# Three dilations of an attention phase taken in another order, and stores issued on a second DMA queue

## The chip, the cores and the metric

The kernel runs on one core of one Trainium2 chip. The metric is the device time of one execution in microseconds (us); three executions give a median of 2603.55 us, from 2603.17 to 2605.61 us.

## What is computed

The reference is a trunk of two layers over 1024 tokens of width 1024. Each layer is a mixer with a residual, then a SwiGLU feed-forward block with a residual. The change touches only the mixer of the second layer, `mixer_cd`, which has two kinds of heads side by side:

```python
hq, hf, hi, hg, sq, sk, sv = split_cols(h @ w_in, CD_SPLITS)
o_c = hgrn2_recurrence(silu(hq), k_in, hi, log_f)          # 4 heads, chunkwise recurrence
o_c = rms_norm(o_c, norm_g) * sigmoid(hg)
sq, sk = rope(sq, pos), rope(sk, pos)                      # 3 patterns x 4 heads
for p, (window, dilation) in enumerate(((128, 1), (512, 4), (2048, 16))):
    o_p, lse_p = dilated_window_attention(sq[:, :, p], sk[:, :, p], sv[:, :, p], window, dilation)
wts = softmax(stack(lses))                                 # over the three patterns
o_d = sum over p of o_p * wts_p
return concat([o_c, o_d]) @ w_out
```

So each of the four attention heads has three outputs, one per pattern, and they are combined with weights from their softmax sums. In the code and below the patterns are p = 0, 1, 2 (dilations 1, 4, 16), and "dilation p" is the one of pattern p.

## The kernel before, in words

All matrix products in 32 bits are made of three products of a high and a low half (`mm3`, L123). TensorE (PE) runs them nearly without a break; everything else is arranged around PE's order of instructions, which inside `mixer_cd` is the order of the program text (`manual_schedule`, L2216). The order on the other engines and on SyncE's DMA queue (SP) is set by the compiler's scheduler, which goes by its own estimate of when each instruction is ready. Each queue works strictly in its order once it is set.

The phase has a main stream of projections: `hgrn_v` (values of the recurrence, twice 8 row tiles), `swa_v(p)` (values of dilation p, for all heads), `swa_qk` (queries and keys of dilation 1, one head), `hgrn_gates` (twice 4 tiles), and `leading` (nine pieces of the output projection, of six matmuls each, that need only the first six of eight inputs). Queries and keys of the dilations 0 and 2 were projected in an earlier phase and lie in DRAM (`pairs.qk`), not yet turned by rope.

Between pieces of the main stream `tick(cost)` (L2195) puts in steps of two other generators: it adds cost times a rate to a counter for each and runs one step for each full unit. `hgrn_v` costs 1 per tile, `swa_v` 16 in all, `swa_qk` 8, `hgrn_gates` 8 per half, `leading` 0.5 per piece. `chain` is the recurrence (rate 0.7). `local` (L2153) is the attention: a unit `Attend(h, p)` has four steps n, each of two blocks of 128 queries. One call of `local` does `scores` of step n, `flip` (transposes) of the step before and `outputs` of the one before that, so a unit's results are complete two calls after its last scores. Its softmax lies on VectorE (DVE) and ScalarE (ACT), L2017 and L2018.

The order before is: `swa_v(1)`; `swa_qk` of heads 0 and 1; `hgrn_v` second half; `swa_qk` 2 and 3; `swa_v(2)`; `swa_v(0)`; gates; leading. Units of dilation 1 become ready after each `swa_qk` (rate 0.7), the four of dilation 2 only after `swa_v(2)`, the four of dilation 0 only after `swa_v(0)`, both at rate 1.0 (L2225 to L2228):

```python
for p in (2, 0):
    swa_v(p, tick)
    ready += [(h, p, None) for h in range(4)]
    rate[0] = 1.0
```

A unit of dilation 0 or 2 is set up one unit ahead (`load`, L1960): k and q come in from DRAM, a second copy `rs` with the halves of the head exchanged comes in by two DMAs each (L1986, L1987), and four turns of three DVE operations on 128x512 (`part`, L1967) do the rope. The table of cosines is loaded by `turn` (L1898), and again for dilation 0. For dilation 1 the rope follows the projection directly (L1923, L1924) and frees its PSUM bank.

Values go from PSUM through an ACT copy to the tile `sw` and by SP to DRAM (`scr_v`, L1885; `scr_h`, L1700); scaled outputs of the recurrence go to `scr_g` (L1833). All DMAs are on SP. Outputs of the dilations 1 and 2 go to `scr_o`. When a unit of dilation 0 ends a group g of four blocks, `combine` (L2096) loads the other two (`cm`, L2101), mixes the three on DVE and ACT, and two calls of `local` later transposes the result on PE (L2131) and stores it to `cat` (L2134). The output projection after the phase loads `cat` again (`cin`, L1084) and splits it into halves; the leading pieces lack the inputs 6 and 7 of `cat[0]`, which are the attention heads 2 and 3.

## Time and profile before

| | before |
|---|---|
| median of 3 executions | 2603.55 us |
| the profiled execution, its own time | 2600.88 us |
| its span in the profile | 2599.1 us |
| PE busy | 2555.1 us, 98% |
| DVE busy | 1662.7 us, 64% |
| ACT busy | 1033.5 us, 40% |
| DMA, share of 16 engines in hardware queues | 53.3% |
| granted clock of PE, mean | 0.996 |

The profile counts PE as busy while a matmul runs, and matmuls overlap; so what matters for this kernel is the little time in which PE is not busy, what ended each such wait, and the stretches in which PE was granted less than its full clock. Times within the span are given as us from its start; `mixer_cd` lies between about 1390 and 1875 us.

### The profile page before, as it was taken

The page shows a single profiled execution, that of the slowest core. Times are in us where ns is not written, and L with a number is a line of the kernel's source. Part 1 is how long each engine was busy: PE and PEld are TensorE (multiplying, and loading weights), DVE is VectorE, ACT ScalarE, POOL GpSimd, SP SyncE. Part 2 cuts the span into 40 slices and gives each one's busy share as a digit, 9 for nine tenths or more (in the row PEclk, how much of TensorE's full clock was granted, in tenths as well). Part 3 has the DMA queues.
Part 4 walks back from the last instruction along what each step waited for, and adds up shares of the span by engine and source line. Part 5 has one row for each costly group of instructions (what it writes and reads, how often), then busy time and mean ns, then how long its engine had stood idle before and what let it go on. Part 6 is the DMA issues. An engine that isn't in the chain of part 4 may idle for free. (4 is left out here: it accounts for less than half of the span.)

```text
span 2599.1 us, 37598 instructions
## 1 busy us (share of the span) xinstructions
PE 2555.1 (98%) x14179; PEld 2129.6 (82%) x14179; DVE 1662.7 (64%) x2814; ACT 1033.5 (40%) x1855; POOL 514.4 (20%) x440
## 2 busy tenths in 40 slices
PE   8999999999999999999999999998999999999998
PEld 6888888888888888888888898877788888888887
DVE  7887776585656665567665457567767565566554
ACT  5432123343333344344443555454544333334442
POOL 1110121334342300024330000000023433331001
PEclk9999999999999999999999999999999999999999
DMA  4434446424556688533326424578762555668853
GB/s 143 137 100 151 123 144 202 167 84 167 176 190 203 222 284 289 193 126 121 132 98 196 125 90 111 153 187 230 244 216 68 172 177 196 205 209 279 275 183 120
DMA packets 279510, 447.63 MB, mean 172 GB/s; under 512 B 49152, under 2 KB 140064, under 8 KB 279200
## 3 DMA queue, kind: packets, MB, share of 16 engines
q1 hardware_dynamic: 279328, 445.23, 53.3%
q8 instruction: 111, 1.82, 0.3%
q14 instruction: 71, 0.58, 0.1%
HBM read 307.16 MB, written 137.97 MB: 171 GB/s over the span
## 5 line engine op out<-in xcount | busy, mean ns | idle before, releaser
L103 DVE TENSOR_TENSOR w<-raw,w 128x1024 fp32r<-128x1024 f32 (+1 forms) x319 | 381.5, 1198 | 155.8 <-ACT w L102 155.0
L102 ACT CAST w<-raw 128x1024 fp32r<-128x1024 f32 (+1 forms) x319 | 306.8, 963 | 280.8 <-PE psu L128 140.4
L126 PE MATMUL psu<-hnh,w 128*128 128x512 f32 x888 | 355.3, 400 | 7.3 <-ACT w L102 7.3
L128 PE MATMUL psu<-hnh,w 128*128 128x512 f32 x888 | 347.8, 392 | 0.0
L127 PE MATMUL psu<-hnl,w 128*128 128x512 f32 x888 | 347.6, 391 | 0.0
L126 PEld LDWEIGHTS psu<-hnh,w 128*128 128x128 f32 x888 | 167.7, 189 | 41.4 <-ACT w L102 7.7
L128 PEld LDWEIGHTS psu<-hnh,w 128*128 128x128 f32 x888 | 167.4, 189 | 36.3 <-DVE w L103 0.8
L127 PEld LDWEIGHTS psu<-hnl,w 128*128 128x128 f32 x888 | 167.8, 189 | 33.9 <-DVE hnl L2253 0.6
L187 POOL TENSOR_TENSOR acc<-acc,sq 128x512 f32<-128x512 f32 x48 | 69.7, 1453 | 517.4 <-ACT sq L183 400.2
L302 POOL TENSOR_TENSOR ws<-raw 128x512 f32<-128x512 f32 x50 | 73.9, 1478 | 421.5 <-DMA raw<-in_dram 232.2
L103 DVE TENSOR_TENSOR w<-ws,w 128x1024 fp32r<-128x1024 f32 x47 | 61.7, 1313 | 118.5 <-ACT w L102 118.5
L103 DVE TENSOR_TENSOR hidq<-hr,hidq 128x1024 fp32r<-128x1024 f32 x72 | 82.1, 1141 | 76.0 <-ACT hidq L102 75.5
L102 ACT CAST hidq<-hr 128x1024 fp32r<-128x1024 f32 x72 | 70.2, 979 | 100.0 <-DMA hr<-ts 61.1
L126 PE MATMUL psm<-hidq,w 128*128 128x512 f32 (+1 forms) x275 | 106.0, 385 | 0.0
L127 PE MATMUL psm<-hidq,w 128*128 128x512 f32 (+1 forms) x275 | 105.8, 385 | 0.0
L128 PE MATMUL psm<-hidq,w 128*128 128x512 f32 (+1 forms) x275 | 105.8, 385 | 0.0
L126 PE MATMUL psu<-t3h,w 128*128 128x512 f32 x224 | 87.3, 390 | 1.0 <-ACT u L365 1.0
L126 PE MATMUL psu<-t4h,w 128*128 128x512 f32 x224 | 87.5, 391 | 0.5 <-ACT c L372 0.5
L128 PE MATMUL psu<-t4h,w 128*128 128x512 f32 x224 | 87.2, 389 | 0.0
L127 PE MATMUL psu<-t4l,w 128*128 128x512 f32 x224 | 87.2, 389 | 0.0
L127 PE MATMUL psu<-t3l,w 128*128 128x512 f32 x224 | 87.1, 389 | 0.0
L128 PE MATMUL psu<-t3h,w 128*128 128x512 f32 x224 | 87.1, 389 | 0.0
(489 smaller groups left out, 6476.8 us busy)
## 6 DMA issues: line engine op xcount, KB each, us to landing
raw<-in_dram SPq DMA_DIRECT2D x227, 512.0 KB, 4.0
sd<-in_dram SPq DMA_DIRECT2D x44, 512.0 KB, 3.9
hid<-hid SPq DMA_DIRECT2D x88, 256.0 KB, 2.7
sd<-sd SPq DMA_DIRECT2D x44, 512.0 KB, 3.3
hr<-ts SPq DMA_DIRECT2D x40, 512.0 KB, 4.9
raw<-sd SPq DMA_DIRECT2D x40, 512.0 KB, 4.2
hd<-h SPq DMA_DIRECT2D x48, 256.0 KB, 3.5
h<-hd SPq DMA_DIRECT2D x48, 256.0 KB, 5.6
```

The source lines that it names most:

```text
L102: S.copy(hi, src)
L103: eng.tensor_tensor(lo, src, hi.bitcast(F32), op=SUB)
L126: T.matmul(o, lh, rh, start=first and i == 0, stop=False, **kw)
L127: T.matmul(o, lh, rl, start=False, stop=False, **kw)
L128: T.matmul(o, ll, rh, start=False, stop=last and i == n - 1, **kw)
L187: (eng or G).tensor_tensor(a, a, q, op=ADD)
L302: G.tensor_tensor(s[:, HT:], b[:, :HT], b[:, HT:], op=ADD)
```

## The change

The units are taken in another order. The values are projected in the order `swa_v(2)`, `swa_v(1)`, `swa_v(0)`; units of dilation 2 are ready from the start, `swa_qk` of head 0 stands before `swa_v(0)` and those of heads 1 to 3 behind it, with units of dilation 0 between them. The rate of `local` is 0.47 from the second `hgrn_v` on and 0.68 after `swa_v(0)`; that of `chain` is 0.72. A third generator, `turns` (rate 0.38), does the rope of dilation 0 in 16 items of half a head's q or k: it loads, turns and stores to new DRAM tensors `final`, from which the units of dilation 0 load q and k ready-made. Units of dilation 2 load their exchanged copies one quarter at a time, from a ring of four half-size tiles `rs`. As a head's dilation 0 can now end before its dilation 1, its output may go to `scr_o` too, and `combine` then loads all three. A counter `made` keeps the units and the head being projected within the two buffers of q and of k. Stores of `scr_h`, `scr_v`, `scr_g` and of the combined outputs to `cat` are issued on ACT's DMA queue (`store`).

The diff, cut:

```diff
@@ -56,6 +56,7 @@
...
+    store = nc.scalar.dma_start
...
@@ -1651,7 +1652,7 @@
...
-        scr_o = dr.tile([4, 2, T_LEN, 132], F32, name="scr_o")
+        scr_o = dr.tile([4, 3, T_LEN, 132], F32, name="scr_o")
...
@@ -1697,7 +1698,7 @@
                 def put(tt, o):
...
-                    dma(scr_h[tt * P:(tt + 1) * P, pair * 256:(pair + 1) * 256], t)
+                    store(scr_h[tt * P:(tt + 1) * P, pair * 256:(pair + 1) * 256], t)
...
@@ -1830,7 +1831,7 @@
...
-                    dma(scr_g[half, h].rearrange("p (c t) -> p c t", c=4), go)
+                    store(scr_g[half, h].rearrange("p (c t) -> p c t", c=4), go)
...
@@ -1868,8 +1869,7 @@
...
-            def swa_v(p, tick):
+            def swa_v(p, tick, groups):
...
@@ -1882,9 +1882,9 @@
                 def put(tt, o):
...
-                    dma(scr_v[p][tt * P:(tt + 1) * P, :], vs)
-                for tts in ((0, 1, 2), (3,), (4,), (5, 6, 7)):
+                    store(scr_v[p][tt * P:(tt + 1) * P, :], vs)
+                for tts in groups:
...
@@ -1893,22 +1893,52 @@
...
-            table = {}
-            def turn(p):
-                if (p == 0) not in table:
-                    table.clear()
-                    t = table[p == 0] = tl("turn", (2, T_LEN))
-                    if p:
-                        dma(t[:, :, 0:320], c_rope[:, :, T_LEN:])
-                    else:
-                        dma(t, c_rope[:, :, 0:T_LEN])
-                return table[p == 0]
+            turn12 = tl("turn12", (2, 320))
+            dma(turn12, c_rope[:, :, T_LEN:])
+            final = [dr.tile([2, P, 2, HT], F32, name=f"fin{h}") for h in range(4)]
+            def exchanged(i, b, src):
+                x = tl("rs", bufs=4)
+                dma(x[0:64], src[i, 64:128, b])
+                dma(x[64:128], src[i, 0:64, b])
+                return x
+            def rotated(c, x, cos, sin):
+                V.tensor_tensor(x, x, sin, op=MULT)
+                V.tensor_tensor(c, c, cos, op=MULT)
+                V.tensor_tensor(c, c, x, op=ADD)
+            def turns():
+                prepare()
+                for _ in range(4):
+                    yield
+                    ahead[0].turn(1)
+                items = [(h, i) for h in range(4) for i in range(2)]
+                for half in range(NH):
+                    t = tl("turn0", (2, HT))
+                    dma(t, c_rope[:, :, half * HT:(half + 1) * HT])
+                    held = {}
+                    def load(n):
+                        if n < len(items):
+                            h, i = items[n]
+                            c = tl("rs", bufs=4)
+                            dma(c, pairs.qk[0, h][i, :, half])
+                            held[n] = c, exchanged(i, half, pairs.qk[0, h])
+                    load(0)
+                    for n, (h, i) in enumerate(items):
+                        load(n + 1)
+                        c, x = held.pop(n)
+                        rotated(c, x, t[:, 0], t[:, 1])
+                        dma(final[h][i, :, half], c)
+                        yield
...
             def swa_qk(h, tick):
...
-                w, turns = wload(("cd", 20 + h), ("cd", 32 + h)), turn(1)
+                w = wload(("cd", 20 + h), ("cd", 32 + h))
...
@@ -1947,45 +1977,49 @@
...
                 def __init__(self, h, p, qk):
...
-                    self.todo = []
+                    self.todo, self.asks = [], []
                     if p == 1:
...
                     else:
-                        self.load(turn(p), pairs.qk[p, h])
-                    self.vp = values(h, p)
+                        self.load(pairs.qk[p, h])
+                    self.vp = None
...
-                def load(self, turns, src):
+                def load(self, src):
...
+                    if self.p == 0:
+                        dma(self.k, final[self.h][1])
+                        dma(self.q, final[self.h][0])
+                        return
...
                     def streams(ap):
-                        return ap.rearrange("p (s i) -> p s i", s=16) if self.p else ap
-                    def part(c, x, b):
-                        for y, t in ((x, 1), (c, 0)):
-                            if self.p:
-                                t = turns[:, t, None, 256 + b * 32:288 + b * 32].to_broadcast([P, 16, 32])
-                            else:
-                                t = turns[:, t, b * HT:(b + 1) * HT]
-                            V.tensor_tensor(y, y, t, op=MULT)
-                        V.tensor_tensor(c, c, x, op=ADD)
-                    for i, t in ((1, self.k), (0, self.q)):
-                        if self.p and i == 0:
-                            c4 = t.rearrange("p b t -> p (b t)").rearrange("p (s b i) -> p b s i", s=16, b=2)
-                            cs = [c4[:, b] for b in range(2)]
-                            for b in range(2):
-                                dma(cs[b], src[i, :, b].rearrange("p (s i) -> p s i", s=16))
-                        else:
-                            cs = [streams(t[:, b]) for b in range(2)]
-                            dma(t, src[i])
-                        x = tl("rs", (2, HT), 2)
-                        dma(x[0:64], src[i, 64:128])
-                        dma(x[64:128], src[i, 0:64])
-                        self.todo += [lambda c=cs[b], y=streams(x[:, b]), b=b: part(c, y, b) for b in range(2)]
+                        return ap.rearrange("p (s i) -> p s i", s=16)
+                    def ask(c, i, b):
+                        x = streams(exchanged(i, b, src))
+                        cos, sin = (turn12[:, t, None, 256 + b * 32:288 + b * 32].to_broadcast([P, 16, 32])
+                                    for t in range(2))
+                        self.todo.append(lambda: rotated(c, x, cos, sin))
+                    c4 = self.q.rearrange("p b t -> p (b t)").rearrange("p (s b i) -> p b s i", s=16, b=2)
+                    dma(self.k, src[1])
+                    for b in range(2):
+                        dma(c4[:, b], src[0, :, b].rearrange("p (s i) -> p s i", s=16))
+                    for i, cs in ((1, [streams(self.k[:, b]) for b in range(2)]), (0, [c4[:, b] for b in range(2)])):
+                        self.asks += [lambda c=cs[b], i=i, b=b: ask(c, i, b) for b in range(2)]
+                    for _ in range(2):
+                        self.asks.pop(0)()
+                def turn(self, n):
+                    for _ in range(n):
+                        if self.todo:
+                            self.todo.pop(0)()
+                        if self.asks:
+                            self.asks.pop(0)()
...
@@ -2075,11 +2109,16 @@
...
-                    if p == 0:
-                        late.append(combine(h, g, ol, sums))
+                    ended.add((h, p, g))
+                    if p == 0 and (h, 1, 1) in ended:
+                        late.append(combine(h, g, (ol, sums)))
...
-                    if p == 1:
+                    if p == 0:
+                        V.tensor_copy(ol[:, :, P:w], sums)
+                        dma(scr_o[h, 2, g * HT:(g + 1) * HT].rearrange("(j i) d -> i j d", i=P)[:, :, 0:w],
+                            ol[:, :, 0:w])
+                    elif p == 1:
...
@@ -2092,11 +2131,16 @@
...
-            def combine(h, g, ol, sums):
-                t, st = [ol], [sums]
-                for p in range(2):
+                    if p == 1 and g and (h, 0, 1) in ended:
+                        late.extend(combine(h, i) for i in range(2))
+            def combine(h, g, own=None):
+                if own is None:
+                    for _ in range(1 + 2 * g):
+                        yield
+                t, st = ([own[0]], [own[1]]) if own else ([], [])
+                for p in range(2) if own else (2, 0, 1):
...
@@ -2131,7 +2175,7 @@
...
-                dma(catd[g][4 + h], go)
+                store(catd[g][4 + h], go)
...
@@ -2148,34 +2192,34 @@
...
-            ready, late, diag, holding, combined = [], [], [], [0], [0]
+            ready, late, diag, holding, combined, made, ended = [], [], [], [0], [0], [0], set()
+            unit, ahead = [], []
+            def prepare():
+                if ready and not ahead and len(unit) // 2 + made[0] < 2:
+                    ahead.append(Attend(*ready.pop(0)))
...
             def local():
...
-                line, now, ahead = [None, None], [], []
-                def prepare():
-                    if ready and not ahead:
-                        ahead.append(Attend(*ready.pop(0)))
+                line = [None, None]
                 while True:
                     nxt = None
+                    now = unit
...
-                    if now and ahead and now[1] > 1:
-                        for turn_part in ahead[0].todo[:2]:
-                            turn_part()
-                        del ahead[0].todo[:2]
+                    if now and ahead and now[1]:
+                        ahead[0].turn(now[1] // 3 + 1)
...
-                        for turn_part in ahead[0].todo:
-                            turn_part()
+                        ahead[0].turn(4)
...
+                        now[0].vp = values(now[0].h, now[0].p)
...
                     if now:
                         nxt = tuple(now)
...
-                            now = []
+                            now.clear()
...
@@ -2188,13 +2232,13 @@
...
-            hg_chain, loc = chain(), local()
-            works = (loc, hg_chain)
-            due, rate = [0.0] * 2, [0.0, 0.7]
+            hg_chain, loc, turner = chain(), local(), turns()
+            works = (loc, hg_chain, turner)
+            due, rate = [0.0] * 3, [0.0, 0.72, 0.38]
...
             def tick(cost):
...
-                for i in range(2):
+                for i in range(3):
...
@@ -2202,12 +2246,16 @@
...
+            tokens = (0, 1, 2), (3,), (4,), (5, 6, 7)
             def query_keys(hs):
...
-                    while len(ready) + holding[0] > 1:
+                    while holding[0] > 1:
...
-                    ready.append((h, 1, swa_qk(h, tick)))
-                    rate[0] = 0.7
+                    made[0] = 1
+                    qk = swa_qk(h, tick)
+                    made[0] = 0
+                    ready.insert(0, (h, 1, qk))
...
@@ -2215,17 +2263,24 @@
...
+                ready += [(h, 2, None) for h in range(4)]
+                next(turner)
...
-                swa_v(1, tick)
-                query_keys((0, 1))
+                rate[1] = 0.72
+                swa_v(2, tick, tokens)
+                rate[0] = 0.47
...
-                query_keys((2, 3))
-                for p in (2, 0):
-                    swa_v(p, tick)
-                    ready += [(h, p, None) for h in range(4)]
-                    rate[0] = 1.0
+                swa_v(1, tick, tokens)
+                query_keys((0,))
+                swa_v(0, tick, tokens)
+                for _ in turner:
+                    pass
+                ready += [(h, 0, None) for h in range(2)]
+                rate[0] = 0.68
+                query_keys((1, 2, 3))
+                ready += [(h, 0, None) for h in (2, 3)]
...
```

## Rows read from the trace of the kernel before

**Rows 1.** Windows of five stretches: us, busy time of each engine, granted clock, DMA share, GB/s.

```profile
core 0: us, PE busy (x) PEld busy (x) DVE busy (x) ACT busy (x) POOL busy (x), PEclk, DMA share, GB/s
1390.00:1624.00 234.00, 231.64 (x2352) 202.89 (x2350) 127.96 (x319) 115.08 (x306) 5.31 (x5) 1.00 0.42 120
1624.00:1633.30 9.30, 6.35 (x141) 4.82 (x140) 4.99 (x11) 1.47 (x6) 0.00 (x0) 0.63 0.70 172
...
1759.00:1773.30 14.30, 7.66 (x31) 6.16 (x31) 7.34 (x21) 3.04 (x14) 1.01 (x1) 0.76 0.93 210
1773.30:1870.00 96.70, 89.53 (x497) 74.56 (x496) 78.13 (x293) 51.64 (x145) 0.00 (x0) 1.00 0.79 235
...
sum 510.00, PE 488.23 PEld 414.75 DVE 310.88 ACT 250.72 POOL 14.91; mean PE 69.75 PEld 59.25 DVE 44.41 ACT 35.82 POOL 2.13
```

**Rows 2.** Waits of PE, 1390 to 1900: us in total, times, longest us.

```profile
PE psm L2011 <- issue: 6.6, 1, 6.6
PE psu L2131 <- DVE ol L2124: 3.1, 4, 2.0
PE psu L126 <- DVE k L1924: 2.9, 1, 2.9
PE psm L2011 <- DVE k L1924: 2.4, 2, 1.8
PE psm L2043 <- ACT e L1832: 1.7, 1, 1.7
PE psm L2058 <- DVE pt L2060: 1.2, 1, 1.2
PE psm L2058 <- DVE w L2119: 1.2, 1, 1.2
PE psm L2011 <- DVE stat L2017: 1.1, 1, 1.1
```

**Rows 3.** Timeline of PE at 1769: start us, us, instruction, idle before it.

```profile
1768.94 1.62 PE L2011 MATMUL psm<-k,q 128*128 128x128 f32 x4 [6.64 <-issue]
```

**Rows 4.** Timeline of DVE at 1621 to 1627 and at 1767.

```profile
1621.31 1.28 DVE L1973 TENSOR_TENSOR q<-q,turn 128x512 f32<-128x512 f32 x2
...
1626.06 1.02 DVE L1924 TENSOR_TENSOR k<-psu,sw 128x512 f32<-128x512 f32 x1
...
1766.94 1.29 DVE L1973 TENSOR_TENSOR rs<-rs,turn 128x512 f32<-128x512 f32 x2 [3.12 <-DMA rs<-qk]
```

**Rows 5.** Timeline of SP at 1761.

```profile
1760.91 0.56 SPq L1885 DMA_DIRECT2D scr_v<-sw  x1
1761.52 0.48 SPq L1987 DMA_DIRECT2D rs<-qk  x1
```

**Rows 6.** Waits of SP, 1390 to 1900: us in total, times, longest us.

```profile
SPq L1885 <- ACT sw L1884: 55.5, 18, 11.4
```

**Rows 7.** DMA issues, 1390 to 1900: count, KB each, median us to landing.

```profile
raw<-in_dram SPq DMA_DIRECT2D x33, 512.0 KB, 4.5
rs<-qk SPq DMA_DIRECT2D x32, 256.0 KB, 4.7
```

**Rows 8.** Line L1885: ns min/median/max of the issue, first and last start.

```profile
L1885 SPq DMA_DIRECT2D scr_v<-sw x24: 319/320/2715, 1428.9 to 1760.9; - x24
```

**Rows 9.** Timeline of PE at the phase's end.

```profile
1861.40 0.59 PE L2131 MATMUL psu<-cf,ol 128*128 128x128 f32 x2 [0.47 <-DVE ol L2124]
...
1869.98 0.30 PE L2131 MATMUL psu<-cf,ol 128*128 128x128 f32 x1 [1.98 <-DVE ol L2124]
...
1874.17 0.39 PE L127 MATMUL psg<-hnl,w 128*128 128x512 f32 x1
```

**Rows 10.** Timeline of SP at the phase's end.

```profile
1863.16 0.33 SPq L2134 DMA_DIRECT2D cat<-sw  x1
1866.85 1.78 SPq L1084 DMA_DIRECT2D cin<-cat  x4
```

**Rows 11.** Timeline of DVE at the phase's end.

```profile
1871.06 1.29 DVE L103 TENSOR_TENSOR hnl<-cin,hnh 128x512 fp32r<-128x512 f32 x2
```

More of the change, by code (lines that the diff above doesn't have):

```diff
@@ L1922, in swa_qk @@
                         for y, t in ((x3, 1), (o3, 0)):
-                            V.tensor_tensor(y, y, turns[:, t, half * P:(half + 1) * P, None].to_broadcast([P, P, 4]), op=MULT)
+                            V.tensor_tensor(y, y, turn12[:, t, half * P:(half + 1) * P, None].to_broadcast([P, P, 4]), op=MULT)
                         V.tensor_tensor(z[:, half].rearrange("p (r i) -> p i r", r=4), o3, x3, op=ADD)
```

## The prediction, made before the change was timed

> **What bounds the kernel now.** I read the stages first, then PE's waits, then the timeline around each long wait, engine by engine, until something was found that had really been late. In the windows [rows 1] PE is busy 488.2 of the 510.0 us that hold the phase; the 21.8 us in which it is not, and two stretches of low clock, are all that this change can touch, because it leaves every matmul in place. In 1624 to 1633 the granted clock is 0.63 and in 1759 to 1773 it is 0.76: full speed but for some 6.9 us at half speed (1.2 instead of 2.4 GHz), each worth 9.3 x 0.37 = 14.3 x 0.24 = 3.4 us. Both follow a long wait of PE, of 2.9 and 6.6 us [rows 2]; no wait of 2 us or less has such a stretch behind it. So the most there is to win is 21.8 + 6.8 = 28.6 us, or 1.1%. Waits [rows 2] sort into five places: (A) first scores of a dilation 1 unit waiting for its rope, 2.4; (B) `swa_v(2)` wanting three PSUM banks while rope of the last `swa_qk` still holds one, 2.9; (C) units of dilation 2, whose steps come so close that the flip waits for the softmax, 1.7 and three small ones, 2.6 in all; (D) the first scores of dilation 0, 6.6; (E) waits on DVE in the gates, 1.2 + 1.2 + 1.1 and small ones, 4.1; (F) transposes of the last combines, 2.0 + 0.5.
>
> D is put down to "issue", so I followed it back. PE starts at 1768.94 [rows 3]; DVE had waited 3.1 us for the exchanged copy of q and taken it at 1766.94 [rows 4]. SP had issued that copy only at 1761.52, right behind the store of a value tile at 1760.91 [rows 5]. SP works in order, and that store waits for ACT's copy of a bank that PE had just finished. Over the phase SP waited 55.5 us in 18 such places [rows 6].
>
> **The change part by part.** *The order of steps.* I walked the ticks through both versions. Before, `swa_v(0)`, gates and leading give 16 + 16 + 4.5 = 36.5 ticks at rate 1.0 for eight units: 32 calls, 2 to finish the last outputs, 2 for its combine, 36 in all. After, 48 ticks at 0.47 (22.6 calls) hold the four units of dilation 2 and the first of dilation 1; `swa_qk` 1 to 3, gates and leading give 24 + 16 + 4.5 = 44.5 ticks at 0.68, 30.3 calls, for seven units, which want 28 + 4 = 32. The last combine therefore runs past the end of leading.
>
> *A.* Heads 0 to 2 of dilation 1 now start 9 to 20 us after their projection. Head 3 starts one gate piece behind it, the cover that before gave waits of up to 1.8. I keep 1.5 of 2.4: gain 0.9 (bounds 0 and 2.4).
>
> *B.* `swa_v` behind `swa_qk` is still there, once. Before, DVE had just spent 2.6 us on q of a dilation 2 unit (four operations, two of them shown) before it came to the rope that PE wanted, done at 1626.06 + 1.02 [rows 4]. After, the rope of dilation 2 is over by then and at most one item of `turns` (3 x 0.64 = 1.9 us) can stand there. Without it PE would wait some 0.5 us, with it up to 2.4; I keep about 1.2 of the wait and one chance in six of the low clock: 6.3 - 1.8 = 4.5 (bounds 0 and 6.3).
>
> *C.* At 0.47 no two calls are adjacent, except the two that `query_keys` forces ahead of head 0. Those two wait as the worst pairs before did: I keep 2.0 of 2.6, gain 0.6.
>
> *D.* Units of dilation 0 have no rope, no table and no `rs` any more; two loads of 512 KB, 4.5 us each to landing for that size [rows 7], come from `final`, whose last store lies some 60 us earlier. Both loads can go out while `swa_v(0)` runs, since the value stores are no longer ahead of them on SP. I keep 0.5 of 6.6 + 3.4: gain 9.5 (bounds: 10.0, and 3 if the loads go out only with the unit).
>
> *E.* DVE is 81% busy in 1773 to 1870 78.1 of 96.7, [rows 1]. From these 96.7 us go rope for three units (36 operations of 0.64, 23 us) and some of the combines, which spread over 175 us: below 65%. Part of that load goes to the stretch of `swa_qk` 1 to 3. I keep 2.0 of 4.1: gain 2.1 (bounds 0 and 4.1).
>
> *F, the price.* From the transposes of the last head's first group to its input being split for the output projection there are 10.3 us: transposes at 1861.40 [rows 9], store at 1863.16 and reload at 1866.85 [rows 10], low half done by 1871.06 + 0.64 [rows 11]. Six leading pieces lay in between, and the first matmul after them, at 1874.17 [rows 9], had no wait. By the walk only two pieces are left behind those transposes. PE then has 2 x 1.4 us of leading, 2.1 us of matmuls with input 6 (nine), and 1.4 us of transposes: 6.3 us. It waits 10.3 - 6.3 = 4.0 us instead of 2.5, and with 4 chances in 10 of a low clock (3.4) the loss is 1.5 + 1.4 = 2.9 (bounds 0 and 7.5).
>
> *The stores.* 56 of them move. SP's issue takes 0.32 us [rows 8]; if ACT's costs the same it is 17.9 us on an engine that is busy 250.7 of 510 [rows 1], so it need not show. The worst place is behind a group of three value tiles, where the third copy comes 0.64 us later, six times: 3.8 us at most, nothing at least, as a bank is wanted only in turn. I take 0.3. The trace of before has no DMA on ACT.
>
> *What is added.* The 16 items move 16 x 3 x 256 KB = 12.6 MB, and the units load 4.2 MB where they loaded 8.4: 8.4 MB more, with some 64 more DMA issues on SP (against 56 fewer). Most falls in 1390 to 1624, where DMA is 42% busy at 120 GB/s; 21 MB more there with the rope loads of dilation 2 makes it about 73%, less than the 79% of the gates now [rows 1]. The DVE work is the same 16 x 3 operations. What I can't see is how SP's order copes with a ring of four `rs` tiles that `turns` and the units share: a load that waits for its tile holds up the weights behind it. Bounds 0 and 10; with the stores' 0.3 I take 2.7, nearer the lower end, because that stretch waited only 2.4 us of 234 so far.
>
> **Sum:** 0.9 + 4.5 + 0.6 + 9.5 + 2.1 - 2.9 - 2.7 = 12.0 us. The profiled execution's own 2600.88 becomes 2588.9; it was 2.7 us below the median, so the median goes from 2603.55 to about **2591**. A difference of 0.2%, 5.2 us, is about what a measurement of this kernel can tell from none.
>
> **A rule against the stores.** The rows show SP held for 55.5 us by copies that were not ready [rows 6], which is waiting in order and no transfer. The Trainium skill ("DMA: Bandwidth & Descriptors", section "Issuing engines are not separate DMA queues") says that DMAs of all issuing engines run on the same 16 DMA engines, so that a second issuing engine saves only the time of initiating. By that rule the moved stores would give nothing that PE sees; the trace so far speaks for the waiting.
>
> **The rivals.**
> - *The stores do not matter* (chance 0.09). What makes the loads of the first unit of dilation 0 late is the transfer and their place in the program, directly before the scores, and not the stores ahead of them on SP. D then gives 2 instead of 9.5: 2599. For it: the DMA engines are 93% busy in 1759 to 1773 [rows 1]; against it: the issue at 1761.52 is itself late [rows 5]. This is what the rule of the Trainium skill comes to here.
> - *The waits only move* (0.14). B stays whole (4.5 lost), the end waits 4 us longer still and surely falls to the low clock (2.0 above the 1.4 counted): 2591 + 10.5 = 2601.5, no change that can be measured. For it: the cover at the end really shrinks from six pieces to two; against it: D has a cause that is gone.
> - *Slower: the ring of `rs` holds SP, and SP the weights* (0.11). Each start of `swa_v(1)`, `swa_qk` 0 and `swa_v(0)` lies within the run of `turns`. If a weight load waits there until DVE has turned an item, PE waits for landing (4.5, [rows 7]) and, as at 1627, runs on at half clock (3.4), some 8 us at each. From two such places on, all but the price at the end is eaten; with all three, and a full 7.5 us at the end, it is 2591 + 24 - 2.7 + 4.6 = 2617, with two 2609. For it: SP's waits are long already [rows 6]; against it: none of PE's waits [rows 2] is for weights.
> - *All of it goes* (0.05): only the 4.0 at the end stays of 28.6, so 2603.55 - 24.6 = 2579.
>
> The forecast itself has 0.61, from 2583 to 2597. **The range** 2579 to 2603 holds it, the gain of everything, the first two rivals in most of their spread, and leaves out the slower one and the edges: 0.61 + 0.03 + 0.08 + 0.09, about 0.8. Faster by over 0.2%, below 2598.3: 0.61 + 0.05, a third of the first rival (0.03) and three tenths of the second (0.04), 0.73; within 0.2%: the rest of these two, 0.16; slower: 0.11.
>
> **What the next profile should show.** PE's waits: no L2011 of several us behind "issue"; L2131 or the first matmul with input 7 waiting about 4 us near the end, and this the longest wait. Granted clock: one stretch or none at half speed in the phase. DVE in the gates between 50 and 65%. SP's waits for ACT's value copies gone from SP. A wait of PE for weights (L126 behind ACT or DVE `w`) between 1440 and 1600, or rows of `final` loads issued just ahead of the first scores of dilation 0, would make the prediction wrong.

## The result, and the profile after

The changed kernel takes 2611.6 us (median of 10 executions, 2606.6 to 2616.8), the kernel before 2606.0 us beside it. The ratio is **1.0026**, 95% interval 1.0017 to 1.0034: slower by 0.26%, where 0.5% faster was forecast. The profiled execution has 2609.3 us, its span 2607.5 us (before 2600.9 and 2599.1); where the phase begins, at about 1391, the two traces lie 0.7 us apart (the changed kernel's has one more stretch at half clock, 1.2 instead of 2.4 GHz, at 1164), and behind the phase they run alike. So the phase holds the loss, and its two halves tell different things. The windows of the kernel before (columns as in [rows 1]):

```profile
1390.00:1600.00 210.00, 207.64 (x2218) 182.28 (x2216) 108.33 (x269) 100.44 (x264) 4.04 (x4) 1.00 0.41 121
1600.00:1922.00 322.00, 302.09 (x2253) 250.20 (x2252) 213.92 (x660) 159.95 (x451) 14.43 (x12) 0.98 0.73 206
```

and of the changed kernel, first the halves and then the stretches with a low clock:

```profile
1390.00:1600.00 210.00, 195.65 (x1992) 168.42 (x1991) 138.25 (x368) 91.29 (x276) 4.04 (x4) 0.95 0.78 228
1600.00:1930.00 330.00, 318.51 (x2478) 267.38 (x2477) 187.79 (x565) 169.34 (x438) 16.25 (x12) 0.99 0.51 162
...
1434.00:1444.50 10.50, 5.99 (x19) 4.66 (x19) 8.08 (x18) 4.53 (x13) 0.00 (x0) 0.67 0.90 273
...
1498.00:1512.30 14.30, 10.83 (x187) 9.43 (x185) 7.97 (x30) 6.17 (x20) 0.00 (x0) 0.88 0.40 130
...
1569.00:1584.50 15.50, 9.41 (x56) 7.36 (x55) 12.62 (x50) 12.96 (x45) 0.00 (x0) 0.67 0.83 253
...
1760.00:1874.00 114.00, 110.74 (x692) 94.27 (x691) 65.42 (x246) 57.25 (x161) 1.01 (x1) 1.00 0.54 167
1874.00:1916.00 42.00, 37.00 (x154) 28.52 (x153) 21.69 (x29) 16.84 (x24) 9.38 (x6) 0.96 0.84 290
```

What the clock costs is the length of a stretch times what its granted clock lacks to 1. In the first half PE stands idle 14.4 instead of 2.4 us, and the clock costs 10.5 x 0.33 + 14.3 x 0.12 + 15.5 x 0.33 = 10.3 us where it cost nothing: 22.3 us worse. In the second half PE stands 11.5 instead of 19.9 us, and the clock costs 42 x 0.04 = 1.7 instead of 6.8: 13.5 us better. The difference, 8.8, is near what the spans show (8.4). PE's waits name the places (1390 to 1600, then 1600 to 1930; the answers to [rows 2]):

```profile
PE psu L127 <- ACT sw L1884: 4.5, 1, 4.5
PE psm L2077 <- ACT sc L2071: 4.3, 2, 2.2
PE psm L2063 <- DVE stat L2070: 2.2, 2, 1.9
PE psu L127 <- ACT sw L1700: 1.7, 1, 1.7
...
PE psu L127 <- ACT w L103: 3.5, 2, 1.9
PE psm L2045 <- DVE k L1954: 1.7, 1, 1.7
PE psu L127 <- DVE k L1954: 1.5, 1, 1.5
PE psm L2045 <- DVE stat L2051: 1.0, 1, 1.0
PE psm L2045 <- DMA q<-fin: 0.9, 1, 0.9
PE psg L127 <- ACT hnh L103: 0.8, 1, 0.8
```

The longest wait, at 1434.7, can be followed through DVE, ACT and PE (timeline of the changed kernel):

```profile
1431.61 0.69 DVE L1910 TENSOR_TENSOR rs<-rs,turn 128x512 f32<-128x512 f32 x1 [0.43 <-DMA rs<-qk]
1434.68 0.69 DVE L1909 TENSOR_TENSOR rs<-rs,turn 128x512 f32<-128x512 f32 x1 [2.38 <-DMA rs<-qk]
...
1435.49 0.42 DVE L1714 TENSOR_TENSOR kd<-kd,f 128x256 f32<-128x256 f32 x1
...
1436.00 0.45 ACT L1711 COPY m<-kd 128x256 f32<-128x256 f32 x1 [6.12 <-DVE kd L1714]
...
1438.53 1.07 ACT L1884 COPY sw<-psu 128x512 f32<-128x512 f32 x2
...
1439.17 0.79 PE L127 MATMUL psu<-w,hnh 128*128 128x512 f32 x1 [4.51 <-ACT sw L1884]
```

DVE stands at a rope tile of `turns` that has not landed; the recurrence's `kd` is ready behind it; ACT waits for `kd` with the copies of value tiles behind that; and PE wants the bank that those copies free. This is the picture with which the experiments began, and it turned out to be too small.

The stretch from 1569 to 1584.5 is another matter. There `query_keys`, before it lets the queries and keys of head 0 be projected, runs calls of `local` until at most one unit is held; three calls stand right behind one another, with no projection in between. They are called the forced calls below. They are part of PE's order, which is written in the kernel.

### The profile page after: what moved, and what is told of

It reads as the page before. It is cut to its first block, busy times and chain, and to the rows that moved or that the text cites. A ratio compares the mean times of both kernels' runs of the same rounds, so it can differ in the third digit from the quotient of the medians.

```text
span 2607.5 us, 37671 instructions
## 1 busy us (share of the span) xinstructions
PE 2560.1 (98%) x14179; PEld 2133.8 (82%) x14179; DVE 1668.7 (64%) x2816; ACT 1033.8 (40%) x1855; POOL 514.4 (20%) x440
## 4 chain that ended last, share of the span: by engine, by line
PE 85%; DVE 7%; DMA 4%; ACT 2%; issue 2%; SPq 1%; POOL 0%; ACTq 0%; DVEq 0%; POOLq 0%
PE psu L127 16%; PE psu L129 16%; PE psu L128 16%; PE psg L127 6%; PE psg L128 6%; PE psg L129 6%; PE psm L129 4%; PE psm L128 4%; PE psm L127 4%; DMA rs<-qk 1%; DMA raw<-in_dram 1%; PE psm L2103 1%; DMA cm<-scr_o 1%; DVE h L224 1%; PE psm L2045 1%
## 5 line engine op out<-in xcount | busy, mean ns | idle before, releaser
L127 PE MATMUL psu<-hnh,w 128*128 128x512 f32 x888 | 356.0, 401 | 10.1 <-ACT w L103 10.1
L127 PEld LDWEIGHTS psu<-hnh,w 128*128 128x128 f32 x888 | 168.5, 190 | 44.7 <-ACT w L103 11.0
L303 POOL TENSOR_TENSOR ws<-raw 128x512 f32<-128x512 f32 x50 | 73.8, 1475 | 423.0 <-DMA raw<-in_dram 266.3
L127 PE MATMUL psm<-hidq,w 128*128 128x512 f32 (+1 forms) x275 | 106.0, 385 | 0.0
L127 PE MATMUL psu<-t3h,w 128*128 128x512 f32 x224 | 87.2, 389 | 1.0 <-ACT u L366 1.0
L127 PE MATMUL psu<-t4h,w 128*128 128x512 f32 x224 | 87.5, 391 | 0.5 <-ACT c L373 0.5
```

What stands on the lines that cost most here:

```text
L127: T.matmul(o, lh, rh, start=first and i == 0, stop=False, **kw)
L303: G.tensor_tensor(s[:, HT:], b[:, :HT], b[:, HT:], op=ADD)
```

## The experiments

Each ratio is against the kernel before on the same chip. The compiler's scheduler, called the planner below, lays the order of DVE, ACT and SP; only PE's is written in the kernel.

### Which part costs: the queue, or the order that came with it

Two edits are one line each, and a third kernel alters only the rate of the units:

```diff
 # stores_sp, on the changed kernel
-    store = nc.scalar.dma_start
+    store = nc.sync.dma_start
 # before_act_stores, on the kernel before; likewise scr_h, scr_g and catd
-                    dma(scr_v[p][tt * P:(tt + 1) * P, :], vs)
+                    store(scr_v[p][tt * P:(tt + 1) * P, :], vs)
 # no_forced_calls, on the changed kernel
-                rate[0] = 0.47
+                rate[0] = 0.55
                 hgrn_v(1, wload(("cd", 10), ("cd", 11)), tick)
                 have_v[0] = 2
                 swa_v(1, tick, tokens)
+                rate[0] = 0.47
                 query_keys((0,))
```

> The changed kernel, with its stores back on SP's queue; the order of the units stays new. Changed kernel so far: median 2611.6, 1.0026 of the kernel before. Theory of the ring (the four `rs` tiles that `turns` and the units of dilation 2 share are issued too late, DVE waits for them at the head of its queue, ACT and PE behind it): the stores are no part of it, SP only gets the copies of value tiles to wait for again, so no gain: 1.002 to 1.005. Theory of ACT's queue (a store on ACT stands behind ACT's other work, so the two `sw` tiles come free late; ACT waited 2 x 9.5 us for them against 2 x 2.1): those waits go back to about 2 each and PE's waits at 1434 and 1510 shrink, 2 to 5 us faster than the changed kernel: 0.9995 to 1.001.

**Measured: 0.9978** (0.9969 to 0.9987), 2597.3 us. That is below what either theory allowed. Half of the gain that the prediction had forecast for the change is there as soon as the stores stay on SP.

> The kernel before with the 56 stores of value tiles, scaled and combined outputs on ACT's queue, and nothing else changed. My step D (the late issue of the loads on SP, held by such stores, is what makes the first scores of dilation 0 wait 6.6 us): this wait falls below 3 and the half clock behind it goes: 0.996 to 0.998 of before. The rival that the stores do not matter: 0.9995 to 1.0005, the wait stays within 1 us of 6.6. Theory of ACT's queue: 1.0005 to 1.002, with ACT waiting more than 10 us for its `sw` tiles.

**Measured: 0.9989** (0.9981 to 0.9997), between the ranges of step D and of its rival: the same move of the stores, alone, gains, and the wait of 6.6 us is gone. It cannot both gain here and cost 0.5% there, unless something else comes with it. What comes with it is the planner: in the traces of `stores_sp` and of the changed kernel, DVE's and ACT's operations stand in another order from about 1413 on.

> The changed kernel with the units' rate at 0.55 instead of 0.47 from `hgrn_v(1)` to the end of `swa_v(1)`, so that `query_keys((0,))` finds at most one unit held and forces no call of `local`. Theory of the forced calls (three calls of `local` right behind one another in 1569 to 1584, 6 us of waits and 10.24 us of half clock): both go, 7 to 11 us less than the changed kernel, 0.998 to 1.000 of before. Theory of the ring: the waits come from late `rs` tiles whatever the order, and closer units want them sooner: 1.0015 to 1.004.

**Measured: 0.9996** (0.9984 to 1.0008). In 1569 to 1584.5 PE is busy 15.4 of 15.5 us at full clock, where the changed kernel had 9.4 at 0.67, so the forced calls were a cost of their own. The wait at 1434 stayed, at 5.6 us. This edit changes PE's order, and the planner laid the rest anew.

To part queue and order, the next kernels pin the order of one kernel onto another. The names of the instructions are the same in both; a list of them for each engine is tied together:

```diff
+    info = mybir.DependencyInfo(mybir.DependencyClass.NoSync, mybir.DependencyReason.DATA)
+    for names in PINNED:               # DVE, ACT without its stores, SP without them
+        for a, b in zip(names, names[1:]):
+            tc.add_manual_dep(ins[b], a, info)
```

> The changed kernel, stores on ACT's queue as in the change, but in the phase DVE's and ACT's operations and SP's other transfers pinned (by dependencies that order them and wait for nothing) to the order that `stores_sp` has. Any edit of the phase makes the planner lay these orders anew, so `stores_sp` (0.9978) differs from the changed kernel (1.0026) in the queue of 56 stores and in the order. If it is the queue: 1.002 to 1.003, with ACT's `sw` waits and PE's wait of 4 us near 1435 there as in the changed kernel. If it is the order: 0.997 to 0.999, and PE's longest waits are those of `stores_sp` (2.8, 2.6, 2.2).

**Measured: 0.9974** (0.9964 to 0.9983).

> The other cross of the two: stores on SP's queue, the rest pinned to the order of the changed kernel. If it is the queue: 0.997 to 0.999. If it is the order: 1.002 to 1.003, with PE's wait of 4 to 5 us near 1435, behind a DVE that stands at an `rs` tile not landed while `kd` is ready behind it, and half clock after it.

**Measured: 1.0083** (1.0068 to 1.0098), with waits of 5.4, 5.3 and 3.5 us. It is the order. With the queue of the change and the order of `stores_sp` the change gains 0.26%; in the order that it got, SP's queue would have cost still more. Where the order tells, and where it does not, is seen when the first half is cut ahead of the forced calls, first in the changed kernel and then in `act_queue_sp_order`:

```profile
1390.00:1560.00 170.00, 161.74 (x1715) 140.98 (x1714) 108.62 (x279) 70.41 (x205) 3.03 (x3) 0.97 0.79 231
1560.00:1600.00 40.00, 33.91 (x279) 27.44 (x278) 29.64 (x89) 20.88 (x72) 1.01 (x1) 0.87 0.77 215
...
1390.00:1560.00 170.00, 166.89 (x1847) 145.32 (x1845) 114.39 (x289) 70.61 (x209) 3.85 (x6) 1.00 0.83 238
1560.00:1600.00 40.00, 32.13 (x313) 26.05 (x312) 28.62 (x93) 24.07 (x77) 1.31 (x1) 0.87 0.72 208
```

Ahead of the forced calls, idle time and clock cost 8.3 + 5.1 = 13.4 us in the changed kernel, and 3.1 + 0 in the order of `stores_sp`, the better one (0.6 in the kernel before). At the forced calls they cost 6.1 + 5.2 = 11.3 and 7.9 + 5.2 = 13.1: the better order takes nothing off them. Each of these figures is of one execution.

One half of the same cross was run in the kernel before:

> The kernel before with the 56 stores on ACT's queue and all the rest pinned to the order of the kernel before: what the stores alone are worth in the old order of units. My step D: the first scores of dilation 0 wait under 3 instead of 6.6 us, without the half clock behind them, while the wait B (2.9) with its half clock stays: 0.996 to 0.998. Rival that the stores do not matter: 0.9995 to 1.0005 and a wait of 6 to 7 us in the same place. `before_act_stores`, whose order was laid anew, came to 0.9989.

**Measured: 0.9994** (0.9986 to 1.0002), no difference that can be told, and the wait of 6.6 us [rows 2] is still 5.8. With the later pairs (below), all that the queue does in one and the same order is this:

| order laid for | stores on ACT | stores on SP |
|---|---|---|
| the kernel before | 0.9994 | 1 |
| the changed kernel | 1.0026 | 1.0083 |
| `stores_sp` | 0.9974 | 0.9978 |
| `sp_no_forced` | 0.9969 | 0.9970 |
| `end_sp` | 0.9970 | 0.9958 |

From the second row to the third, the same units in another order, the time moves by 0.52% and 1.05%; across a row by 0.12% or less, but for the changed kernel's own order. In that one, with the stores on SP, SP stood 21.1 us in 13 places (1390 to 1600) at stores whose copy ACT had not made yet (12.2 in `stores_sp`); that this is the whole of the 0.57% is not shown. No kernel was pinned to its own order with nothing else changed; the rows with little between their two sides leave little room for a cost of pinning.

### What in that order costs

> The changed kernel with every order pinned to its own, but for four operations of DVE: near 1431 the two pairs of L1738 and L1714 (one halves `kd`, one `qd`, for the levels of an HGRN unit) go ahead of the two rope operations L1910 and L1909, of which L1909 stood 2.4 us at a tile that had not landed. Theory of the order: PE's wait of 4.5 us there falls to 1 or 2 and the 6.8 us at half clock behind it go, 5 to 7 us in all: 0.9995 to 1.001 of before (changed kernel 1.0026). Theory that the place is only one symptom (DVE, ACT or SP is late there anyway, because of the ring or the DMA engines): the wait stays over 3 us or shows up within 20 us behind it, 1.002 to 1.003.

```diff
 DVE: L1909, L1911 (rope of the item before)
+     L1738, L1714 kd, L1738, L1714 qd
      L1910 (rope), L1909 (rope; the tile had not landed)
-     L1738, L1714 kd, L1738, L1714 qd
```

**Measured: 1.0029** (1.0021 to 1.0038). The edit did what it was made for: PE's wait for these copies is 0.2 us, and the 6.8 us at half clock behind it are gone. Yet the time is no shorter. Forty microseconds on, a new wait stands (timeline of `one_place`, ACT and PE):

```profile
1475.32 1.04 ACT L103 CAST w<-raw 128x1024 fp32r<-128x1024 f32 x1 [3.51 <-DMA raw<-in_dram]
1476.28 0.58 ACT L1782 COPY e<-psg 128x512 f32<-128x512 f32 x1
...
1476.90 0.94 PE L1797 MATMUL psg<-vt,e 128*128 128x128 f32 x6 [2.95 <-ACT e L1782]
```

and in the changed kernel itself SP's issues that lead to the same cast of weights, and the cast, read:

```profile
1463.24 0.59 SPq L1904 DMA_DIRECT2D rs<-qk  x1
1466.91 0.44 SPq L1903 DMA_DIRECT2D rs<-qk  x1
...
1469.25 0.34 SPq L116 DMA_DIRECT2D raw<-in_dram  x1
...
1475.34 1.05 ACT L103 CAST w<-raw 128x1024 fp32r<-128x1024 f32 x1 [3.48 <-DMA raw<-in_dram]
```

The weights land at 1475.3 in both. In the changed kernel PE came to them late, because it had waited at 1434, and so found them there. In this order the wait at 1434 does not set the time by itself: the landing of a transfer does, and a shorter wait in one place is a longer one at the next.

> The changed kernel with two rings of `rs`: `turns` takes the three tiles of the combines, which are free until it is over, and one of its own; the units of dilation 2 have two. Theory of the ring: SP's loads no longer wait for the other user's tiles, DVE's waits for `rs` fall from 34.1 us in 17 to under 20, PE's long waits of 1434, 1498 and 1510 go with the half clock behind them: 0.998 to 1.000. If the transfers are late whatever the ring: waits for `rs` stay over 25 us and the time is 1.002 to 1.003. If the order decides, the time can come out on either side, with the long waits in other places.

```diff
-                x = tl("rs", bufs=4)
+                x = tl("rs", bufs=2)                # units of dilation 2
-                            c = tl("rs", bufs=4)
+                            c, x = own(n % 2 * 2), own(n % 2 * 2 + 1)    # cm0, cm1 / cm2, rt
```

**Measured: 1.0021** (1.0010 to 1.0031). DVE's waits for rope tiles, now of three names, come to 28.0 instead of 34.1 us (1390 to 1600):

```profile
DVE cm L1915 <- DMA cm<-qk: 11.3, 6, 4.3
DVE rs L1914 <- DMA rs<-qk: 9.9, 9, 2.9
...
DVE cm L1914 <- DMA cm<-qk: 4.6, 4, 1.8
...
DVE rt L1914 <- DMA rt<-qk: 2.2, 3, 1.6
```

and PE's wait at 1434 is 4.5 as before. That the ring is shared is not the cause. The tiles are as few as they were, and SP stands as long at rope loads until a store of `turns` has landed (17.3 us in 1390 to 1560 in both kernels). More tiles have no room: with four of its own for `turns`, the tiles of the phase (`own_ring`) come to 67.2 KB per partition, and 63.7 are left.

> The changed kernel (stores on ACT, rate 0.47), where each rope of `turns` is put behind the 40 operations of DVE emitted before it (issue order alone; no wait). `one_place` moved one such rope and got the 4.5 us back, but lost them again at 1474 and later. Theory that DVE's order does it in many places (rope whose tile has not landed in front of `kd`, softmax and state operations): the waits for `rs` no longer hold those, and the time falls to what the better order gave, 0.996 to 0.9985. Theory that the rope's supply is what is late (loads behind a ring of four, each pair behind a store that must land, on DMA engines 80 to 90% busy): the rope only gets later, `turns` is not over when `swa_v(0)` ends, and PE waits there instead: 1.001 to 1.004.

```diff
+                ahead_of = [last 40 instructions of DVE emitted so far]
                 V.tensor_tensor(x, x, sin, op=MULT)      # each of the two with a
                 V.tensor_tensor(c, c, cos, op=MULT)      # NoSync dependency on all of them
```

**Measured: 1.0039** (1.0027 to 1.0051). DVE's waits go over to other transfers (1390 to 1600),

```profile
DVE rs L1910 <- DMA rs<-qk: 16.5, 7, 5.4
DVE qd L1742 <- DMA q<-bkq: 10.1, 3, 6.2
```

and PE's wait at 1434 is 4.5 again. What holds `kd` there now is `q<-bkq` and two ropes of a dilation 2 unit (k 1.9, q 1.5 us), which this edit left in front. So it does not yet tell the theories apart, and the last run moved those as well.

> `rope_behind` (1.0039) put only the ropes of `turns` behind what DVE had been given before; near 1430 its trace shows DVE at ropes of a dilation 2 unit (1.9 us for `k`, 1.5 us for `q`) and at `q<-bkq` (6.2), with `kd` still behind them. Here the ropes of the units go behind too, stores on ACT, rate 0.47. If DVE's order decides: no rope stands in front of the recurrence at 1434, PE's wait there goes, and the time falls below 0.999. If the transfers are late in any order of DVE: the wait at 1434 or its follower at 1475 stays with 2 us or more, and the ropes of dilation 2, now later, make the first scores of their units wait: 1.002 to 1.006.

**Measured: 1.0010** (1.0000 to 1.0019), between the two theories. The wait at 1434 is gone, the one at 1475 is 1.5 us, and the scores that start at 1519.4 in the changed kernel start 9.9 us sooner in this one. Then it is all lost at the forced calls, where scores and transposes of dilation 2 wait longer, with their ropes now later on DVE (waits of PE, 1390 to 1600):

```profile
PE psm L2065 <- DVE stat L2072: 4.5, 1, 4.5
PE psm L2065 <- issue: 3.9, 1, 3.9
PE psm L2079 <- ACT sc L2073: 3.2, 2, 2.7
```

with 13.7 us at half clock beside them. The two stretches, to be held against 13.4 and 11.3 us in the changed kernel, read

```profile
1390.00:1560.00 170.00, 168.42 (x1853) 146.78 (x1851) 107.73 (x277) 71.29 (x208) 4.45 (x6) 1.00 0.80 226
1560.00:1600.00 40.00, 27.37 (x284) 22.57 (x285) 31.40 (x95) 21.42 (x72) 1.32 (x1) 0.83 0.79 232
```

that is 1.6 us ahead of the forced calls and 12.6 + 6.8 = 19.4 at them. So ropes that stand in front on DVE are what costs in the first stretch; SP stands there nearly as long as in the changed kernel (79.4 for 82.4 us in all), though its order and ACT's were laid anew too. The forced calls cost the rest. This edit together with the rate of 0.55 was not run.

> The same with the rate of 0.55 up to `query_keys((0,))`. If the two places are apart: 0.002 to 0.003 less than `rope_behind`, 0.994 to 0.997 if that gained. If the closer units of dilation 2 only want their rope sooner: no more than 0.001 less.

**Measured: 1.0024** (1.0014 to 1.0034), 0.0015 below `rope_behind`. Of the 0.002 to 0.003 expected if the two places are apart, somewhat over half came.

> `earlier_end` (0.9975) with the rate of `turns` 0.31 instead of 0.38: its 16 items of three transfers spread over the whole time up to the end of `swa_v(0)`, with the same work. Theory that the rope's supply is late because too much is to be moved and held at once in 1391 to 1600 (DMA engines 88% busy in 1391 to 1434): DVE's waits for DMA there fall from 44 to some 30 us, PE's wait of 4.7 at 1434 falls, 2 to 5 us less: 0.9955 to 0.9967. Theory that only the order laid out matters: no direction, 0.995 to 1.001, and `turns_faster` may as well be the better one.

**Measured: 0.9975** (0.9966 to 0.9984), the same as `earlier_end`.

> The opposite: `earlier_end` with the rate of `turns` 0.46. Theory of the supply: DVE's waits for DMA in 1390 to 1600 grow beyond 50 us, 2 to 6 us more: 0.998 to 1.000. Theory of the order alone: no direction, 0.995 to 1.001.

**Measured: 0.9997** (0.9988 to 1.0006), 0.0022 more, with DMA 93% busy in 1391 to 1434 (88% in the other two) and DVE's waits for DMA at 48.7 us against 44.1 and 44.7. The edit is one number, `rate[2]`. The faster `turns` costs; one slower than the change has brings nothing, and the wait at 1434 stays near 5 us in all three. So the theory of supply holds in one direction at most, and not even that is shown: the order was laid anew here too, and 0.0022 is less than a new order alone has done.

### What the change is worth with a better order

These combine the edits above: `sp_no_forced` has those of `stores_sp` and `no_forced_calls`; `earlier_end` has that of `no_forced_calls` and one more rate; `end_sp` is `earlier_end` with its stores on SP. Of the two pinned ones, `act_no_forced_pinned` has the order of `sp_no_forced` and `end_act_pinned` that of `end_sp`, with the stores on ACT.

> Both single edits that gained: stores on SP and the units' rate 0.55 up to `query_keys((0,))`. `stores_sp` still has 10.2 us of half clock and waits of 2.8, 1.9 and 0.6 at the forced calls. If what the edits gained adds up (0.0048 and 0.0030 of the time): 0.994 to 0.996. If each merely drew another order from the planner: anywhere in 0.996 to 1.002, not below either.

**Measured: 0.9970** (0.9957 to 0.9983): the two gains do not add up to the 0.995 hoped for. It is better than `stores_sp` (0.9978) by less than the intervals, though the forced calls are gone from its trace (0.5 us idle in 1560 to 1600 and no half clock).

> The change with the units' rate at 0.55 up to `query_keys((0,))`, stores on ACT's queue, the rest pinned to the order of `sp_no_forced` (0.9970). In the order of `stores_sp` the queue of ACT was worth 0.0004, in that of the changed kernel 0.0057, more the longer DVE and SP stood. Theory that the change gains by both of its parts once the order is kept: 0.9955 to 0.997, below both kernels. Theory that ACT's queue costs where its copies are wanted: 0.9975 to 0.999, with PE's wait of 2.9 for `sw` near 1435 longer.

**Measured: 0.9969** (0.9957 to 0.9981), the same as with the stores on SP.

> The changed kernel with 0.55 up to `query_keys((0,))` and 0.72 instead of 0.68 for the rest, so that one more leading piece lies behind the transposes of head 3's first combine and four instead of two in front of the end. My step F (the cover of the last combine, 2.9 us with a share of a low clock): PE's waits from 1868 to 1880 (0.8 + 1.6 in the changed kernel) go, 1 to 3 us less than `no_forced_calls` (0.9996): 0.9985 to 0.9992. Rival, the closer units want more of DVE there: 0.9995 to 1.0005. A new order from the planner can shift either by as much as the runs so far have shown, 0.002 to 0.005.

```diff
-                rate[0] = 0.68
+                rate[0] = 0.72
```

**Measured: 0.9975** (0.9967 to 0.9984), against 0.9996 without it and more than either theory allowed. PE's waits from 1866 to 1930 in `no_forced_calls` are

```profile
PE psu L127 <- ACT w L103: 4.2, 2, 2.5
PE psu L129 <- DVE w L104: 1.1, 2, 0.5
PE psg L127 <- ACT hnh L103: 0.9, 1, 0.9
```

and none of these three is left in `earlier_end`; 2.1 us in the norm behind the phase take their place. The order was laid anew here too, so not all of the 0.0021 belongs to the end.

> `earlier_end` (0.9975, stores on ACT) with its stores on SP and the order laid anew. In all pairs so far the order that came with the stores on SP was the better one by 0.0026 to 0.0052 (changed kernel 1.0026 and 0.9974, rate of 0.55 0.9996 and 0.9969, both with ACT's queue). If that holds with the earlier end too: 0.994 to 0.996. If the orders are drawn without a rule: 0.995 to 1.001.

**Measured: 0.9958** (0.9946 to 0.9970), 2591.9 us: the lowest of all versions, faster than both kernels.

> The same order as `end_sp` pinned, the stores on ACT's queue: the change with both of its parts, without forced calls and with the earlier end. The third pair of queue and order. ACT's queue was worth 0.0057, 0.0004 and 0.0001 against SP's in the same order, never a loss: here 0 to 0.001 less than `end_sp`, 0.9935 to 0.996. If a store on ACT costs something of its own: more than `end_sp` by 0.001 or over.

**Measured: 0.9970** (0.9961 to 0.9979). ACT's queue does not gain here; of the expectation's two ends it is the second, by 0.0012, with intervals that overlap.

## Why the prediction was wrong

**Two terms of the sum failed, and together they make nearly all of the miss**: 12.0 us of gain were forecast, and the profiled execution is 8.4 slower.

The first is the last term, "what I can't see is how SP's order copes", bounds 0 and 10, taken at 2.7 with the stores' 0.3. In 1390 to 1560, ahead of the forced calls, the loss measured 13.4 us (0.6 before), five times what was taken and above the upper bound. The prediction looked for it in the ring and in weights held up on SP. The runs show the planner's order in its place: in another order of DVE, ACT and SP the same stretch costs 3.1 us, and with the ropes moved behind other work of DVE 1.6.

The second is *C*. The prediction saw the forced calls and kept 2.0 us for them, "as the worst pairs before did", and counted no half clock. They cost 11.3 us, 6.1 of waiting and 5.2 of clock, and the planner's order is not the reason: in the better order they cost 13.1. The rest of the terms, A, B, D, E and F, were forecast at 14.1; the second half, in which they lie but for A's old waits, gained 13.5, the 2.6 of C's old waits among them.

- *A* (dilation 1's first scores): 1.5 of 2.4 kept was forecast, 1.7 is there (L2045 behind `k`). Right.
- *B*: about 1.2 us left and rarely a low clock; the wait is 1.5 (L127 behind `k`), no half clock. Right.
- *C*: wrong, as told above.
- *D*: 6.6 + 3.4 to 0.5, measured 0.9 (`q<-fin`), no half clock. Right in size, wrong in its reason. The stores of value tiles were not what held the rope loads: with them off SP and the order kept, the load is issued at 1761.96 (1761.52 before, [rows 5]), behind a store of dilation 2's outputs that the change does not move, and PE waits on. SP and PE in `before_act_pinned`:

```profile
1760.66 1.25 SPq L2095 DMA_DIRECT2D scr_o<-ol  x2
1761.96 0.62 SPq L1988 DMA_DIRECT2D rs<-qk  x1
...
1769.19 1.62 PE L2012 MATMUL psm<-k,q 128*128 128x128 f32 x4 [5.79 <-issue]
```

  I had read the store just ahead of the late load and not the one ahead of that. That D went because units of dilation 0 need no rope any more, the other reason which the prediction gave, fits the trace and was not tested by itself.
- *E*: DVE was forecast below 65% in the gates and is at 65.4 of 114 us, 57%. Right.
- *F*: 4.0 us of waiting plus 1.4 for the clock were forecast at input 7. The waits there come to 2.9, 0.8 for the input itself and 1.6 and 0.5 for weights whose halves are made behind it. Another 1.9 us for weights and 1.7 of half clock follow at 1909.9, which the prediction did not name. The place was right, the total is 6.5 for 5.4, and over half of that lies elsewhere.
- *What is added*: DMA was forecast about 73% busy in 1390 to 1624, and is at 74%. The share was right; what late transfers do to PE at that share, through a DVE that works in the order laid for it, was not. "That stretch waited only 2.4 us of 234 so far" was an argument from a stretch with half the transfers.

**The rivals.** "The stores do not matter" had 0.09 and is what the pinned pairs show of the queue. The Trainium skill ("DMA: Bandwidth & Descriptors", section "Issuing engines are not separate DMA queues") lets a second issuing engine save only the time of initiating. The runs agree in four kept orders of five (0.9994 in that of the kernel before) and not in the changed kernel's own, where moving the stores off SP took 1.0083 to 1.0026. The slower rival (0.11) had the sign, and one place looks like it: at 1463.8 SP stands 3 us at a rope load (L1903), 2.4 of them until DVE has used the tile, in front of weights that land 3.5 us late for ACT. But that the ring is shared is not what counts (`own_ring_cm`), and at the forced calls none of PE's waits is for weights.

**What stands shown.** The loss has two parts of like size, and the queue of the stores is neither. One is the order that the planner laid for DVE, ACT and SP, in a half that now moves nearly twice the bytes (228 for 121 GB/s): with the same order of PE and the same queue, another such order takes 1.0026 to 0.9974. Where it costs most, ropes whose transfers are late stand in front of ready work on DVE: `one_place`, which moves other work ahead of two of them with all else pinned, takes PE's wait at 1434 from 4.5 to 0.2 us, and `all_ropes_behind` takes the stretch up to 1560 from 13.4 to 1.6. The other is the forced calls, which PE's written order has and which cost 11.3 and 13.1 us in two orders of the planner; at the rate of 0.55 they are gone (`no_forced_calls`).

**What stays open** is how much of the first part is SP's order, and why the two gains do not add up (0.9969 with both, 0.9974 with the order alone). A mix, DVE's order of one kernel with SP's of the other, was not run; that such a program would wait for itself, because tiles are handed round in two different orders, is an argument and no measurement. It is also not shown that the order with stores on SP is better by more than luck; it was so in three of three drawings (by 0.0052, 0.0027 and 0.0005, stores on ACT in both).

## What to carry to other kernels

Where a scheduler lays the order of some engines, an edit has two effects, its own and that of the order laid anew; here the second was up to 0.5% with the queue of the change, larger than what moving the stores did in most kept orders (0.12% or less). Pin the order of one version onto the other before an effect is put down to the edit, and give a prediction this spread as a term of its own. Then cut the time at the places that are written in the program, as the forced calls are: what costs the same in two laid orders is the program's own. And where transfers are late, a long wait of PE that is taken away can come back at the next late transfer: look for the landing that is the same in both traces.

## What the hardware showed beside that

A short wait can have a half clock behind it: the prediction had seen none behind waits of 2 us or less, but in the changed kernel 1.91 us for weights ended at 1911.8 and 3.4 us at half clock (granted 0.50) began at 1912.0. Nor is it the wait alone. Outside the phase, at 1163, PE waits the same 1.9 us in the same code in both profiled executions; 3.4 us at half clock follow in the changed kernel's and none in that of the kernel before. A store that ACT issues takes 0.33 us of its queue (24 at L1885, median 326 ns), as on SP [rows 8].
